# A hybrid decoder step: where one exponential stands, and which PSUM pool holds the running sums

## The chip, the cores and the metric

The kernel runs on one NeuronCore of one Trainium2 chip. The metric is the device time of one execution in microseconds (us); lower is better.

## What is computed

One inference step (512 prompt positions and 8 samples, together 520 columns) of one decoder layer with 1024 channels:

```python
x = x + 0.5 * swiglu(rmsnorm(x, norm_ffn1_w), ...)
h = rmsnorm(x); p = h @ w_in                 # z, x/B/C, dt, three short-conv parts
...
dt = softplus(dt_raw + dt_bias)
A = -exp(a_log)
a = dt * A
acum = cumsum(a, within a chunk)             # the running sums of the decays
y_ssd, S_new = ssd_scan(xs, dt, A, Bm, Cm, ssm0)
...
x = x + concat(y_ssd, y_sc) @ w_out
x = x + 0.5 * swiglu(rmsnorm(x, norm_ffn2_w), ...)
y = rmsnorm(x, final_norm_w)
```

There are 16 heads, so `a_log` holds 16 numbers; on the chip it is laid out as 128 x 16 inside the tile of small parameters `pc`.

## The kernel before

Activations lie with channels on the partitions and the 520 columns in two halves of 260. Every large product is three matmuls (high by high, high by low, low by high part); the split of a weight block into its parts is a cast on ScalarE (ACT, line 148) and a subtraction on VectorE (DVE, line 149). Weights come over SyncE's (SP's) queue into two `raw` buffers; up to four split units wait in `whl`.

The program is three stages: `ffn(1)`, `mixer`, `ffn(2)`. A scheduler of the tile framework orders each engine's instructions when the program is built; `high_priority` moves instructions forward, and the pools hand out their buffers. Nothing of that order is written out by hand.

PSUM has eight banks. In the mixer, pool `mm` holds three pairs of banks (`psum()`), used by the projections, and pool `aux` holds two single banks (`c.bank()`). The mixer begins while `ffn(1)` still ends:

- line 741: the small dt projection, into one pair of `mm` (32 matmuls);
- `nxt.factor()` (lines 304 to 314): two matmuls with ones (line 311) over the sums of squares `acc`, Sqrt on ACT (312), reciprocal on DVE (313). This gives `r`, the norm factor of all columns. The squares come from ACT (299) and are added on GpSimd (POOL, 302);
- `c.table(AF.Exp, r[:, :1])` (lines 316 to 321): a copy of one column of `r` times zero, and an exponential of it whose result is not used. ACT needs its exponential table for it (ACT_TABLE_LOAD);
- the dt chain, under `high_priority(300)`: `dth` (750), five transposes on TensorE (PE, 755), then some twenty small operations on DVE (762 to 787) with one exponential on ACT (767), which make `dt` and `da`. In between, `nega` = exp(a_log) (784), whose inputs are there from the start of the kernel;
- the running sums: matmuls at lines 791 and 792 into `pa`, a single bank, and at 805 and 806 into `ph`; copies to `acs` and `tot` (794, 795); the result goes to DRAM (`scr`, 809), from where the scan loads it (872);
- `conv(i)` for twelve blocks: `project()`, that is 48 matmuls of line 205 into a pair of `mm`, then the causal convolution on DVE and ACT (831 to 845). The scan, the short convolutions and the output projection follow.

The lines that matter, before:

```python
r = nxt.factor()
rv = halves(r)
c.table(AF.Exp, r[:, :1])
with tc.high_priority(300):
    ...
    nega = dp.tile([P, NH], F32, name="nega")
    c0 = _PC["alog"][0]
    S.activation(nega, pc[:, c0:c0 + NH], AF.Exp)
    ...
    pa = c.bank()
```

Of the kernel before, what the change touches and what calls it, by code (L numbers as in the profile page):

```python
# [10 lines left out]
F32 = mybir.dt.float32  # L11
F32R = mybir.dt.float32r
AF = mybir.ActivationFunctionType
# [3 lines left out]
P = 128  # L17
# [8 lines left out]
NH = 16  # L26
# [18 lines left out]
_PC = {}  # L45
# [10 lines left out]
def halves(ap):  # L56
    return ap.rearrange("p (h n) -> p h n", h=2)
# [14 lines left out]
class Core:  # L72
# [199 lines left out]
    def par(self, name, i, n=1):  # L272
        c = _PC[name][0] + i
        return self.pc[:, c:c + n]
# [213 lines left out]
def build(nc, tc, ctx, a, o):  # L488
# [143 lines left out]
    ffn(1, nx1, nxt)  # L632
    nx2 = Blocks(c, x, "n2", ("th", "tl", "xh", "xl"))
    mixer(c, o, x, nxt, nx2)


# [43 lines left out]
def mixer(c, o, x, nxt, nx2):  # L680
    nc, tc, a = c.nc, c.tc, c.a
    V, S, G, PE = c.V, c.S, c.G, c.PE
    par, pc = c.par, c.pc
# [8 lines left out]
    with ExitStack() as c0:  # L692
        ytp = c0.enter_context(tc.tile_pool(name="ytp", bufs=1))
        mmp = c0.enter_context(tc.tile_pool(name="mm", bufs=3, space=bass.MemoryType.PSUM))
        psum = lambda: mmp.tile([P, 2, 512], F32, tag="mm", name="mmt")
# [36 lines left out]
        with tc.tile_pool(name="dp", bufs=1) as dp:  # L732
# [11 lines left out]
            ps = ps[:, :, :H2]  # L744
            r = nxt.factor()
            rv = halves(r)
            c.table(AF.Exp, r[:, :1])
            with tc.high_priority(300):
                dth = dp.tile([NR, T], F32, name="dth")
                V.tensor_tensor(halves(dth), ps[:NR], rv[:NR], op=ALU.mult)  # L750
# [7 lines left out]
                c0 = _PC["dtb"][0]  # L758
                bias = pc[:, c0:c0 + NH]
# [19 lines left out]
                V.scalar_tensor_tensor(dt.rearrange("p c h -> p (c h)"), l1, 2.0, vf, op0=ALU.mult, op1=ALU.add)  # L779


                nega = dp.tile([P, NH], F32, name="nega")
                c0 = _PC["alog"][0]
                S.activation(nega, pc[:, c0:c0 + NH], AF.Exp)
                V.tensor_scalar(nega, nega, -1.0, None, op0=ALU.mult)
                da = dp.tile([P, NT, NH], F32, name="da")
                V.tensor_tensor(da, dt, nega.unsqueeze(1).broadcast_to([P, NT, NH]), op=ALU.mult)
                daf = da.rearrange("p c h -> p (c h)")
                NCF = NCH * NH
                pa = c.bank()  # L790
                PE.matmul(pa[:, :NCF], tri[:, 0], daf[:, :NCF], start=True, stop=True)
                PE.matmul(pa[:, NCF:2 * NCF], c.ones, daf[:, :NCF], start=True, stop=True)
                tot = dp.tile([P, NCH, NH], F32, name="tot")
# [347 lines left out]
```

## Time and profile before

| | |
|---|---|
| median of 3 runs | 1151.43 us (1151.27 to 1152.59) |
| the profiled execution | 1150.9 us, its span 1149.1 us |
| PE busy | 1118.4 us (97%) |
| PE weight loads busy | 1101.3 us (96%) |
| DVE / ACT / POOL busy | 848.4 / 539.8 / 148.6 us |
| mean granted TensorE clock | 0.99 |

The span runs from the first to the last instruction of the profiled execution, 1.8 us less than that execution's own time. Matmul records overlap, since one begins before the last has drained; the distance between starts tells the pace.

### The profile page before, as it was taken

To read this page: it belongs to the slowest core of one execution; us is meant where nothing else is said; L and a number is where in the kernel's file an instruction comes from. 1 tells how busy PE (TensorE), PEld (TensorE's weight loads), DVE (VectorE), ACT (ScalarE), POOL (GpSimd) and SP (SyncE) were. 2 spreads that over 40 slices of the span, in tenths; PEclk is the share of its full clock that TensorE was granted. 3 is DMA by queue.
4 is the path that set the end of the run, shared out by engine and by line. 5 is a ranking of instruction groups with operands and counts; after the bars stand their busy time and mean duration, and the time that the engine had idled before them with its cause. 6 is when DMAs were issued, how large, how long until landed. Compare 5 with 4: busy or idle time off the path is not lost.

```text
span 1149.1 us, 21781 instructions
## 1 busy us (share of the span) xinstructions
PE 1118.4 (97%) x9127; PEld 1101.3 (96%) x9127; DVE 848.4 (74%) x1280; ACT 539.8 (47%) x800; POOL 148.6 (13%) x247
## 2 busy tenths in 40 slices
PE   9799999999999999999999999999999999999994
PEld 8799999999999999999999999999999999999994
DVE  7788778777766675799876676349887778777755
ACT  7454434344435568466443454335544344344442
POOL 1000000000002565422221231120000000000012
PEclk9899999999999999999999999999999999999998
DMA  6123132322233523365542222331323322233223
GB/s 224 38 88 115 65 138 79 115 78 100 90 102 117 151 76 111 121 220 174 202 144 81 80 91 81 105 110 41 108 79 115 126 86 76 96 102 115 82 85 74
DMA packets 47434, 122.97 MB, mean 107 GB/s; under 512 B 9384, under 2 KB 19784, under 8 KB 41832
## 3 DMA queue, kind: packets, MB, share of 16 engines
q1 hardware_dynamic: 47336, 121.58, 32.6%
q8 instruction: 71, 1.16, 0.4%
q14 instruction: 27, 0.22, 0.1%
HBM read 114.43 MB, written 7.14 MB: 106 GB/s over the span
## 4 chain that ended last, share of the span: by engine, by line
PE 75%; DVE 11%; DMA 7%; issue 2%; ACT 2%; POOL 1%; SPq 1%; DVEq 0%; ACTq 0%; POOLq 0%
PE pst L221 30%; PE mmt L205 20%; PE auxt L582 19%; PE pst L256 4%; DMA raw<-in_wu 3%; DVE lo L149 2%; DVE st L961 1%; DMA out_ss<-st 1%; ACT hi L148 1%; DMA st<-in_ssm 1%; DVE S L134 1%; DMA raw<-in_wg 0%; DMA s<-scr 0%; DVE y L672 0%; DMA x<-in_xT 0%
## 5 line engine op out<-in xcount | busy, mean ns | idle before, releaser
L148 ACT CAST hi<-raw 128x1024 fp32r<-128x1024 f32 (+3 forms) x218 | 188.6, 869 | 288.0 <-PE mmt L205 97.7
L149 DVE TENSOR_TENSOR lo<-raw,hi 128x1024 fp32r<-128x1024 f32 (+3 forms) x218 | 219.8, 1011 | 68.8 <-ACT hi L148 65.5
L582 PE MATMUL auxt<-hh,hi 128*128 128x260 f32 x704 | 198.0, 284 | 1.7 <-DVE x L583 1.6
L582 PE MATMUL auxt<-hl,hi 128*128 128x260 f32 x704 | 197.6, 283 | 0.0
L582 PE MATMUL auxt<-hh,lo 128*128 128x260 f32 x704 | 195.1, 283 | 0.3 <-DVE lo L149 0.3
L205 PE MATMUL mmt<-xxh,hi 128*128 128x260 f32 x704 | 146.5, 288 | 0.0
L205 PE MATMUL mmt<-xxh,lo 128*128 128x260 f32 x704 | 144.5, 286 | 0.0
L205 PE MATMUL mmt<-xxl,hi 128*128 128x260 f32 x704 | 143.9, 285 | 0.0
L582 PEld LDWEIGHTS auxt<-hh,hi 128*128 128x128 f32 x704 | 132.2, 188 | 3.1 <-DVE x L583 2.4
L582 PEld LDWEIGHTS auxt<-hl,hi 128*128 128x128 f32 x704 | 132.5, 188 | 0.0
L582 PEld LDWEIGHTS auxt<-hh,lo 128*128 128x128 f32 x704 | 131.0, 188 | 0.6 <-DVE lo L149 0.5
L148 ACT CAST hi<-S 128x1024 fp32r<-128x1024 f32 x78 | 80.8, 1051 | 72.5 <-PE pst L221 43.1
L205 PEld LDWEIGHTS mmt<-xxh,hi 128*128 128x128 f32 x704 | 110.3, 191 | 0.6 <-PE auxt L909 0.2
L205 PEld LDWEIGHTS mmt<-xxl,hi 128*128 128x128 f32 x704 | 110.0, 190 | 0.8 <-issue 0.8
L205 PEld LDWEIGHTS mmt<-xxh,lo 128*128 128x128 f32 x704 | 110.0, 190 | 0.6 <-issue 0.4
L149 DVE TENSOR_TENSOR lo<-S,hi 128x1024 fp32r<-128x1024 f32 x78 | 94.5, 1220 | 16.8 <-ACT hi L148 16.6
L386 ACT ACTIVATE cp<-pst 128x260 f32<-128x260 f32 x117 | 45.0, 386 | 118.7 <-PE pst L221 118.3
L295 POOL TENSOR_TENSOR acc<-x 128x520 f32<-128x520 f32 x4 | 4.4, 1107 | 702.9 <-DVE x L583 680.1
L221 PE MATMUL pst<-fxh,hi 128*128 128x260 f32 x320 | 90.4, 284 | 0.0
L221 PE MATMUL pst<-fxl,hi 128*128 128x260 f32 x320 | 90.1, 282 | 0.0
L134 DVE TENSOR_TENSOR S<-raw 128x1024 f32<-128x1024 f32 x39 | 47.7, 1224 | 56.3 <-DMA raw<-in_wu 29.4
L221 PE MATMUL pst<-fxh,lo 128*128 128x260 f32 x320 | 89.0, 282 | 0.0
(251 smaller groups left out, 2821.2 us busy)
## 6 DMA issues: line engine op xcount, KB each, us to landing
raw<-in_wi SPq DMA_DIRECT2D x45, 512.0 KB, 3.5
raw<-in_wu SPq DMA_DIRECT2D x22, 1024.0 KB, 5.0
raw<-in_wg SPq DMA_DIRECT2D x21, 1024.0 KB, 4.9
raw<-in_wd SPq DMA_DIRECT2D x48, 384.0 KB, 3.2
raw<-in_wo SPq DMA_DIRECT2D x16, 512.0 KB, 3.7
raw<-in_wd SPq DMA_DIRECT2D x16, 256.0 KB, 2.7
st<-in_ssm SPq DMA_DIRECT2D x16, 256.0 KB, 3.5
s<-scr SPq DMA_DIRECT2D x8, 512.0 KB, 5.1
```

The source lines that it names most:

```text
L134: V.tensor_tensor(s[:, 1:3], r[:, 0:4:2], r[:, 3:4].broadcast_to([P, 2, 512]), op=ALU.add)
L148: self.S.copy(hi, src)
L149: self.V.tensor_tensor(lo, src, hi.bitcast(F32), op=ALU.subtract)
L205: self.PE.matmul(ps[:, h, :H2], w[:, k, :], x[:, h * H2:(h + 1) * H2], start=first and n == 0, stop=last and n == 2)
L221: self.PE.matmul(ps[:, :H2], a[:, k, :], b, start=first and k + i == 0, stop=k == n - 1 and i == 2, skip_group_check=True)
L256: self.PE.matmul(ps[h][:, :H2], a, b[:, h * H2:(h + 1) * H2], start=first and n == 0, stop=last and n == 2)
L295: self.G.tensor_tensor(acc, xt, xt, op=ALU.mult)
L386: self.c.S.activation(t, ps[:, :H2], AF.Copy, scale=sign)
L582: PE.matmul(ps[:, :H2], w[:, k, :], v, start=k + n == 0, stop=k == nk - 1 and n == 2)
L961: V.scalar_tensor_tensor(st[:, b], st[:, b], ddc[:, j, 1, k * HB + b:k * HB + b + 1], up[:, b], op0=ALU.mult, op1=ALU.add)
```

## The change

`nega` is computed right behind the norm factor, with a bias that is zero times the first column of `r`, and so can't start ahead of `r`. It takes the place of the dummy exponential. The two matmuls of lines 791 and 792 write into the first bank of a pair of `mm` instead of a bank of `aux`. Lines below the first edit move by up to four numbers: 755 becomes 759, 791 becomes 792, 805 becomes 806, 815 becomes 816.

```diff
             rv = halves(r)
-            c.table(AF.Exp, r[:, :1])
+
+            nega = dp.tile([P, NH], F32, name="nega")
+            zero = dp.tile([P, 1], F32, name="zero")
+            S.activation(zero, r[:, :1], AF.Copy, scale=0.0)
+            S.activation(nega, par("alog", 0, NH), AF.Exp, bias=zero)
             with tc.high_priority(300):
...
-                nega = dp.tile([P, NH], F32, name="nega")
-                c0 = _PC["alog"][0]
-                S.activation(nega, pc[:, c0:c0 + NH], AF.Exp)
                 V.tensor_scalar(nega, nega, -1.0, None, op0=ALU.mult)
...
-                pa = c.bank()
+                pa = psum()[:, 0]
                 PE.matmul(pa[:, :NCF], tri[:, 0], daf[:, :NCF], start=True, stop=True)
```

PE, before, around the matmuls of the norm factor (line 311): `mmt` is a pair of `mm`, `auxt` a bank of `aux`, `xxh` and `xxl` the parts of the normalised input.

```order
L205 MATMUL mmt<-xxh,hi 128x260
L741 MATMUL mmt<-xxl,hi 128x260 x2
L205 MATMUL mmt<-xxh,hi 128x260
L205 MATMUL mmt<-xxl,hi 128x260 x2
L311 MATMUL auxt<-acc,ones 128x260 x2
L205 MATMUL mmt<-xxh,lo 128x260 x2
```

Projections stand before and behind line 311, and go on up to the transposes of line 755 and from there to the running sums, here in the same program:

```order
L205 MATMUL mmt<-xxl,hi 128x260
L791 MATMUL auxt<-da,tri 128x64
L792 MATMUL auxt<-da,ones 128x64
L805 MATMUL auxt<-tri,da 16x256
L806 MATMUL auxt<-tri,da 16x128
L805 MATMUL auxt<-tri,da 16x256
L806 MATMUL auxt<-tri,da 16x128
L205 MATMUL mmt<-xxl,hi 128x260
```

PE in the changed program, from the end of the dt projection to the first matmul of any projection:

```order
L741 MATMUL mmt<-xxl,hi 128x260 x2
L311 MATMUL auxt<-acc,ones 128x260 x2
L759 MATMUL auxt<-idn,dth 128x48 x4
L759 MATMUL auxt<-idn,dth 8x48
L792 MATMUL mmt<-da,tri 128x64
L793 MATMUL mmt<-da,ones 128x64
L806 MATMUL auxt<-tri,da 16x256
L807 MATMUL auxt<-tri,da 16x128
L806 MATMUL auxt<-tri,da 16x256
L807 MATMUL auxt<-tri,da 16x128
L816 MATMUL auxt<-idn,dt 16x8
L205 MATMUL mmt<-xxh,hi 128x260 x2
```

Norm factor, transposes and running sums now stand one behind the other, and the first projection stands behind all of them.

ACT at the same place, before:

```order
L784 ACT_TABLE_LOAD
L784 ACTIVATE nega<-pc 128x16
L338 ACTIVATE xxh<-x_100,pc 128x520
L299 ACTIVATE sq<-x_100 128x520
L148 CAST hi<-raw 128x1024 x2
L312 ACT_TABLE_LOAD
L312 ACTIVATE r<-auxt,eps 128x260 x2
L320 ACTIVATE tbl<-r 128x1
L321 ACT_TABLE_LOAD
L321 ACTIVATE tbl<-tbl 128x1
```

and in the changed program:

```order
L338 ACTIVATE xxh<-x_100,pc 128x520
L299 ACTIVATE sq<-x_100 128x520
L148 CAST hi<-raw 128x1024
L312 ACTIVATE r<-auxt,eps 128x260 x2
L750 ACTIVATE zero<-r 128x1
L751 ACT_TABLE_LOAD
L751 ACTIVATE nega<-pc,zero 128x16
L771 ACTIVATE e<-e 128x80
L814 ACTIVATE dcs<-da 8x16
L801 ACTIVATE dec<-dec 128x64
L802 ACTIVATE cd<-cd 128x32
L148 CAST hi<-raw 128x1024
```

Two table loads and a cast are gone from ahead of the norm factor, and the exponentials of the dt chain follow it directly.

## Rows read from the trace of the kernel before

**Rows 1.** The page's first part: busy time, share of the span, instructions.

```profile
PE 1118.4 (97%) x9127; PEld 1101.3 (96%) x9127; DVE 848.4 (74%) x1280; ACT 539.8 (47%) x800; POOL 148.6 (13%) x247
```

**Rows 2.** PE's waits, whole span: total us, times, longest.

```profile
PE auxt L755 <- ACT tbl L321: 2.2, 1, 2.2
...
PE auxt L921 <- DVE xe L897: 0.8, 1, 0.8
```

**Rows 3.** Timeline of PE: start us, us, engine, line, operation [idle before].

```profile
392.18 0.40 PE L205 MATMUL mmt<-xxh,hi 128*128 128x260 f32 x2
392.42 0.40 PE L205 MATMUL mmt<-xxl,hi 128*128 128x260 f32 x2
...
396.75 0.46 PE L755 MATMUL auxt<-idn,dth 48*128 48x48 f32 x5 [2.23 <-ACT tbl L321]
397.13 0.51 PE L205 MATMUL mmt<-xxh,hi 128*128 128x260 f32 x2
```

**Rows 4.** Line 205 from 378 to 394.6 us: ns min/median/max, first and last start.

```profile
L205 PE MATMUL mmt<-xxl,hi x32: 277/282/286, 381.5 to 394.0; 128*128 128x260 f32 x32
```

**Rows 5.** Timeline of ACT, same columns as rows 3.

```profile
382.40 1.28 ACT L784 ACT_TABLE_LOAD   x1
383.70 0.22 ACT L784 ACTIVATE nega<-pc 128x16 f32<-128x16 f32 x1
383.82 0.71 ACT L338 ACTIVATE xxh<-x,pc 128x520 fp32r<-128x520 f32 x1
...
391.99 0.84 ACT L312 ACTIVATE r<-auxt,eps 128x260 f32<-128x260 f32 x2
...
409.29 0.27 ACT L767 ACTIVATE e<-e 128x80 f32<-128x80 f32 x1
```

**Rows 6.** Timeline: POOL's last sum of squares, and PE's norm factor.

```profile
385.14 1.36 POOL L302 TENSOR_TENSOR acc<-acc,sq 128x520 f32<-128x520 f32 x1 [3.53 <-ACT sq L299]
...
387.47 1.04 PE L311 MATMUL auxt<-acc,ones 128*128 128x260 f32 x4
```

**Rows 7.** Timeline of DVE, from the last split ahead of the norm factor.

```profile
390.71 1.22 DVE L149 TENSOR_TENSOR lo<-raw,hi 128x1024 fp32r<-128x1024 f32 x1 [1.08 <-ACT hi L148]
392.50 3.42 DVE L313 RECIPROCAL r<-r 128x260 f32<-128x260 f32 x2 [0.56 <-ACT r L312]
395.95 0.69 DVE L750 TENSOR_TENSOR dth<-mmt,r 48x520 f32<-48x520 f32 x1
...
410.98 0.64 DVE L770 RECIPROCAL q<-q 128x80 f32<-128x80 f32 x1
...
418.16 0.50 DVE L776 SCALAR_TENSOR_TENSOR l<-l,q 128x80 f32<-128x80 f32 x2
```

**Rows 8.** Timeline of PE at the running sums.

```profile
422.19 0.43 PE L791 MATMUL auxt<-da,tri 128*128 128x64 f32 x2
...
424.19 0.39 PE L205 MATMUL mmt<-xxl,hi 128*128 128x260 f32 x1
```

**Rows 9.** Timeline of PE behind its longest pause, in the first FFN.

```profile
35.91 0.56 PE L256 MATMUL pst<-xxh,hi 128*128 128x260 f32 x1 [5.77 <-DVE g L427]
36.26 0.42 PE L256 MATMUL pst<-xxl,hi 128*128 128x260 f32 x1
36.48 0.42 PE L256 MATMUL pst<-xxh,lo 128*128 128x260 f32 x1
```

**Rows 10.** Stretches: us, busy of PE, PEld, DVE, ACT, POOL; PEclk, DMA share, GB/s.

```profile
33.00:34.00 1.00, 0.00 (x0) 0.00 (x0) 1.00 (x2) 0.00 (x0) 0.00 (x0) 0.59 0.00 0
39.00:40.00 1.00, 1.00 (x7) 1.00 (x6) 0.91 (x3) 0.00 (x0) 0.00 (x0) 0.50 0.00 0
40.00:41.00 1.00, 1.00 (x10) 1.00 (x10) 0.10 (x1) 0.00 (x0) 0.00 (x0) 1.00 0.00 0
390.00:405.00 15.00, 12.77 (x96) 12.49 (x95) 12.47 (x19) 7.50 (x11) 8.54 (x11) 0.89 0.33 108
420.00:440.00 20.00, 20.00 (x149) 18.80 (x148) 13.85 (x28) 15.80 (x25) 12.82 (x29) 0.91 0.42 134
470.00:640.00 170.00, 168.32 (x1392) 160.44 (x1391) 140.17 (x254) 86.15 (x176) 38.91 (x75) 1.00 0.49 159
```

**Rows 11.** ACT's waits for the scan's loads: total us, times, longest.

```profile
ACT s L880 <- DMA s<-scr: 17.1, 5, 5.9
```

## The prediction

> **What bounds the kernel now.** I read the page's engine line first. PE is busy 97% of the span and its weight loads 96%, DVE 74%, ACT 47% [rows 1]: matmuls set the time, and a change moves it by what it adds to or takes from PE's idle time and PE's clock. PE's list of waits came next. Around this change it has one wait of weight, 2.2 us at the transposes of line 755 [rows 2]. In the timeline PE is idle for 2.23 us before them, and a matmul of line 205 follows at 397.13, at the transposes' heels [rows 3]. That matmul needs nothing of what the transposes waited for, yet it did not run in the pause. So PE takes matmuls in their order, and what stands behind a waiting one waits too. Last came the order of the instructions before and after, because the cost of the pause depends on what stands behind it.
>
> Before, projections fill almost all of the time in which ACT, POOL and DVE make the norm factor and the dt chain. Between 378 and 394.6 us line 205 issues three products with 32 matmuls each, one of them shown [rows 4]: 96, which is conv blocks one and two whole. In the changed order every one of these stands behind the running sums. I take the reason to be the second edit: the pair for `pa` is asked for ahead of the pairs of the conv blocks, and the pool serves requests in program order. The order is a fact; its reason is not needed for the sum.
>
> **The first edit, step by step.** The exponential of `a_log` leaves the place where it had its own table load, 1.28 us with 0.1 us more until `xxh` began [rows 5]. The reload for Sqrt and the reload behind it become one load behind the norm factor. So the chain to the norm factor shortens. `xxh` can start at 382.4 instead of 383.8, and POOL's last addition, which started 1.32 us behind `xxh`, at 383.7; it ends 1.36 us later, at 385.1 [rows 5, 6]. The matmuls of line 311, which queued behind projections until 387.47, start at 385.2 and are through 1.04 us later, at 386.2 [rows 6].
>
> From there, on the profile's clock:
> - the two square roots without a load, 0.84 us [rows 5]: about 386.0 to 386.9. DVE first finishes a split of 1.22 us [rows 7] whose cast waits for the end of the dt projection (about 384.9): it ends at 387.2.
> - the two reciprocals, 3.42 us [rows 7]: 390.6. `nega` on ACT needs the first of them (388.9), a copy of 0.2, the load of 1.28 and 0.22 [rows 5]: 390.7, and its negation on DVE some 0.2 us. It now stands ahead of `dth`, but ends almost with the second reciprocal. I charge 0.3 us.
> - `dth`, 0.69 us [rows 7]: 391.6. The transposes begin 0.1 us later and take 0.46 us [rows 3]: 392.2.
> - the dt chain with nothing between its steps. Five small operations, one exponential of 0.27 us [rows 5], one reciprocal of 0.64 us, and thirteen dependent steps at 0.25 us, the pace of the pair at line 776 [rows 7]. With 1.0 us for the first five and 0.1 for two hand-overs: 1.0 + 0.4 + 0.6 + 3.3 = 5.3 us. `da` is ready at 397.5.
>
> **The second edit.** PE reaches the running sums at 397.5 with all work done except those 96 matmuls. Before, it was at the same point, behind the transposes, at about 397.2, with the 96 done. At 0.12 us each (two in 0.24 us [rows 3]) they are worth 11.5 us; with the 0.3 us the delay is **11.8 us**. Seen the other way, PE idles some 14 us between 381.4 and 397.5, against 2.2 us before. No other work covers it. Bounds: 10.8 if the split and `nega` cost nothing, 13.3 if each small step takes 0.06 us more and the matmuls of line 311 run at half pace.
>
> The clock. Behind a pause of 5.77 us the matmuls came 0.22 us apart [rows 9]; the granted clock stood at half (1.2 GHz) from within the pause, 33.4, until 40.0, 4.1 us after the work came back [rows 10]. So each microsecond at half loses 0.45 us. Before, a share of 0.89 in 15 us and of 0.91 in 20 us [rows 10] are 3.3 and 3.6 us at half, 1.5 us lost each: one behind the 2.2 us pause, one behind the 16-column matmuls of line 821. After, PE comes back from a longer pause at half. The running sums, 2.0 us at full pace [rows 8], lose between 0 and 2.0; I take 1.0, the middle, since small matmuls are only partly paced by the clock. The projections behind them lose 0.5 (if 4.1 us count from the running sums) to 1.8 (if from the first projection): 1.2. The fall behind line 822 stays at 1.5, or melts into the first. Sum 3.7 against 3.0: **+0.7**, bounds -1.5 and +3.8 (the upper with one more stretch of 1.5).
>
> Costless edits. The two matmuls of the running sums have the same shape in either bank. The other table loads that go (ten fewer in the whole program) lie on ACT, which PE doesn't wait for there. SP now holds the store of the sums and two scan loads ahead of most `in_wi` loads, but four split units are in hand when the pause begins, 23 us of PE's work at 5.76 us each; if that cover failed, PE would wait for a weight load. The scan's inputs are ready far earlier; PE's waits in the scan's stretch are only 1.7 us of 170 [rows 10], so between 0 and 1.6 us can come back. I take 0.
>
> Sum: 11.8 + 0.7 = +12.5 us on the profiled execution's own 1150.9, so 1163.4. The median of the runs is 0.5 us above that execution: **1164 us**.
>
> A price where row and notes part: the load that leaves the path is 1.28 us, and the next operation starts 0.02 us behind it [rows 5]. The Trainium skill (ScalarE: Activation LUTs, What ACT_TABLE_LOAD costs) gives 2.66 us for a switch, half of it a drain that these rows don't show. By it the chain would be 1.4 us shorter and the sum an estimated 11.1.
>
> **The rivals.**
> 1. *PE is not held up: faster.* The new order's chain would run beside projections, the 2.2 us pause at line 755 would go, and with it the half clock behind it, 1.5 us: 1151.4 - 3.7 = 1147.7. For it: the pause is put down to ACT's dummy exponential [rows 2], and ACT's chain gets shorter by two loads. Against it: this needs a projection ahead of the running sums on PE, and the new order has none. It decides as soon as 12 us of projections can pass. 3%. The Trainium skill's rule to group activations by table set (ScalarE: Activation LUTs, Table sets: the hidden batching unit) speaks for this side; the trace agrees that each set change has its load, but it has them on an engine that is 47% busy.
> 2. *A second pause in the conv stage.* ACT now has scan operations, which wait for loads from `scr` of up to 5.9 us [rows 11], ahead of the first block's convolution; DVE's evacuation of the third block needs that block's buffer, and the three pairs of PSUM run dry. Price up to 5.9 us: 1170. It decides if ACT is late by more than two blocks of projection, 11.5 us; I find about 3 us. 8%.
> 3. *The delay is partly given back*: chain at its lower bound, the scan's 1.6 us returned, no second fall of the clock: 10.8 - 1.5 - 1.6 = +7.7, 1159. 8%.
> 4. *No change at the end*: the order is as shown, but PE's pause had been paid elsewhere before. PE's busy share leaves no such place. 2%.
>
> **How the numbers follow.** The forecast has 79%. The range takes its bounds, without their coinciding extremes, and most of rival 3: 1160 to 1168. Left out are rival 1, rival 4, most of rival 2 and the extreme of rival 3, below 2 in 10 together. A measurement of this kernel can tell about 0.2%, 2.3 us, from no change. Faster by more than that is rival 1, 0.03; within it rival 4, 0.02; slower all else, 0.95.
>
> **What would show it.** In the changed kernel's timeline PE should stand still three times: about 3 us in pieces before line 311, some 5.5 us from there to the transposes at line 759, some 5.3 us from there to line 792. Its waits should name DVE's `dth` or `nega` and DVE's `da`. The granted clock should be at half when line 792 starts and for some 3 to 6 us on. The first `L205` with `mmt` should start near 400. The dt chain from `dth` to `da` should take about 6 us, against 26. From there on every line should lie some 12.5 us later than before, with no new wait. A projection between lines 311 and 792 on the timeline, or a PE pause in the conv stage, would prove me wrong.

## The result, and the profile after

| | before | after |
|---|---|---|
| median of the runs | 1151.70 us (1151.27 to 1152.59, 4 runs) | 1161.67 us (1161.11 to 1163.64, 4 runs) |
| ratio of after to before | | 1.0092, 95% interval 1.0076 to 1.0109 |
| the profiled execution, its span | 1150.9 us, 1149.1 us | 1163.64 us, 1161.8 us |
| mean granted TensorE clock | 0.990 | 0.984 |

The change makes the kernel slower by 10.0 us between the medians; 1164 us had been forecast. The profiled execution of after is the slowest of its four, 2 us above their median. So a second profile of the same kernel (after_again, below) stands beside it where the two differ.

The page of after, first part, against [rows 1]: the engines' work is nearly the same, the span is not.

```profile
PE 1120.3 (96%) x9127; PEld 1101.8 (95%) x9127; DVE 853.2 (73%) x1280; ACT 527.9 (45%) x789; POOL 145.1 (12%) x247
```

PE's waits in the whole span of after (line, what it waited for: total us, times, longest), against [rows 2]:

```profile
PE mmt L792 <- DVE da L788: 5.6, 1, 5.6
...
PE auxt L759 <- issue: 5.0, 1, 5.0
PE auxt L865 <- DVE sn L927: 1.8, 1, 1.8
...
PE mmt L741 <- ACT xxh L338: 1.2, 1, 1.2
...
PE mmt L741 <- DVE xxl L339: 0.8, 1, 0.8
PE auxt L311 <- POOL acc L302: 0.6, 1, 0.6
```

Those of lines 741, 311, 759 and 792 stand in one place; line 759 is line 755 of before, whose 2.2 us have become 5.0, and the others are new there. At line 759 the profile finds no releaser (`issue`); DVE's `dth` ends at 392.78 us (its row is below), 0.1 us ahead of the transposes, which read it. PE's timeline of after (columns as in rows 3), against [rows 3] and [rows 8]:

```profile
383.38 0.51 PE L741 MATMUL mmt<-xxh,hi 128*128 128x260 f32 x2 [1.17 <-ACT xxh L338]
384.68 0.51 PE L741 MATMUL mmt<-xxl,hi 128*128 128x260 f32 x2 [0.79 <-DVE xxl L339]
385.82 2.10 PE L311 MATMUL auxt<-acc,ones 128*128 128x260 f32 x4 [0.64 <-POOL acc L302]
392.88 0.71 PE L759 MATMUL auxt<-idn,dth 48*128 48x48 f32 x5 [4.96 <-issue]
399.19 0.69 PE L792 MATMUL mmt<-da,tri 128*128 128x64 f32 x2 [5.61 <-DVE da L788]
...
403.02 0.80 PE L205 MATMUL mmt<-xxh,hi 128*128 128x260 f32 x2
```

PE stands still for 1.17 + 0.79 + 0.64 + 4.96 + 5.61 = 13.2 us between 382 and 399 us, against 2.23 us before [rows 3]: 10.9 us more, with not one projection of line 205 in between. The first projection comes at 403.02, behind the running sums.

DVE's timeline of after, the chain in these pauses, against [rows 7]:

```profile
386.30 1.23 DVE L149 TENSOR_TENSOR lo<-raw,hi 128x1024 fp32r<-128x1024 f32 x1 [1.67 <-ACT hi L148]
387.60 3.42 DVE L313 RECIPROCAL r<-r 128x260 f32<-128x260 f32 x2
391.27 0.91 DVE L786 TENSOR_SCALAR nega<-nega 128x16 f32<-128x16 f32 x1 [0.25 <-ACT nega L751]
392.10 0.68 DVE L754 TENSOR_TENSOR dth<-mmt,r 48x520 f32<-48x520 f32 x1
...
398.90 0.24 DVE L788 TENSOR_TENSOR da<-dt,nega 128x80 f32<-128x80 f32 x1
```

The dt chain, from the start of `dth` to the end of `da`, takes 392.10 to 399.14, 7.0 us, where DVE has nothing else to do; before it ran from 395.95 [rows 7] until the running sums at 422.19 [rows 8].

Stretches of after (us, busy of PE, PEld, DVE, ACT, POOL; PEclk, DMA share, GB/s), against [rows 10]:

```profile
381.00:386.00 5.00, 2.40 (x16) 1.77 (x15) 2.30 (x4) 2.98 (x4) 2.53 (x5) 0.91 0.96 201
386.00:392.00 6.00, 1.92 (x4) 0.99 (x4) 5.37 (x4) 3.02 (x6) 4.35 (x11) 0.50 0.73 266
...
405.00:406.00 1.00, 1.00 (x7) 1.00 (x8) 0.00 (x0) 0.00 (x0) 0.00 (x0) 0.71 0.00 0
406.00:481.50 75.50, 75.50 (x629) 75.33 (x628) 48.97 (x61) 40.97 (x60) 47.66 (x114) 1.00 0.31 94
```

The clock is at half (1.2 GHz) from within the pauses to 405.6 us. From 406 us to the scan's first matmul at 481.50 PE works without a gap and at full pace. The 16-column matmuls of line 822 stand in this stretch, at 407.80, and no fall of the clock follows them here, as one did behind line 821 before (the 0.91 of [rows 10]).

### The profile page after: what moved, and what is told of

It is laid out like the page before. It is cut to its first block, busy times and chain, and to the rows that moved or that the text cites. A ratio compares the mean times of both kernels' runs of the same rounds, so it can differ in the third digit from the quotient of the medians.

```text
span 1161.8 us, 21776 instructions
## 1 busy us (share of the span) xinstructions
PE 1120.3 (96%) x9127; PEld 1101.8 (95%) x9127; DVE 853.2 (73%) x1280; ACT 527.9 (45%) x789; POOL 145.1 (12%) x247
## 4 chain that ended last, share of the span: by engine, by line
PE 80%; DVE 9%; DMA 7%; ACT 2%; issue 2%; POOL 0%; SPq 0%; DVEq 0%; ACTq 0%; POOLq 0%
PE pst L221 31%; PE mmt L205 22%; PE auxt L582 19%; PE pst L256 4%; DVE lo L149 2%; DMA raw<-in_wu 2%; DMA out_ss<-st 1%; DMA s<-scr 1%; DVE st L962 1%; DMA raw<-in_wg 1%; DMA st<-in_ssm 1%; ACT hi L148 1%; DVE S L134 1%; DVE y L672 0%; POOL acc L302 0%
```

## Experiments

The theory: the second edit asks for a pair of `mm` ahead of the conv blocks, so in program order ahead of their pairs; the pool serves in that order, and the scheduler can no longer put the two blocks' 96 projections ahead of the running sums. PE has nothing to do while ACT, POOL and DVE make the norm factor and the dt chain. The rivals: it is the first edit, by a longer chain; or it is the use of a pair of `mm` for the sums, whoever asks for it.

**One edit alone.** e1_exp_only keeps the exponential's new place and gives `pa` back its bank of `aux`:

```diff
-                pa = psum()[:, 0]
+                pa = c.bank()
```

> Only the first edit: the exponential of a_log behind the norm factor, the running sums in a bank of aux as before. Theory (the pair requested ahead of the conv blocks' pairs holds the projections back): projections stay between line 311 and the running sums, no pause of 5 us on PE. Two table loads less ahead of the norm factor (2 x 1.28 us), so the transposes of line 759 are ready about when PE reaches them: the pause of 2.2 us and the half clock behind it (1.5 us) go, about 1148 us, ratio 0.997, range 0.995 to 1.001. Rival (the exponential's new place with high priority pulls the dt chain forward): as the changed kernel, 1161 to 1164, ratio 1.009.

Measured: 1150.74 us median of 11 runs, ratio to before 0.9994 (0.9980 to 1.0009). No slowdown. PE's timeline has the projections ahead of the transposes again, and a shorter pause than the 2.23 us of [rows 3]:

```profile
394.72 0.41 PE L205 MATMUL mmt<-xxh,lo 128*128 128x260 f32 x2
396.32 0.46 PE L759 MATMUL auxt<-idn,dth 48*128 48x48 f32 x5 [1.19 <-ACT hi L148]
```

The gain that was expected did not reach the end. The first operation of the scan on DVE (the row of its group: ns min/median/max, first and last start) comes at 470.0 us before and at 468.4 here:

```profile
L976 DVE TENSOR_TENSOR t<-mmt,xs x8: 692/699/711, 470.0 to 619.1; 128x520 f32<-128x520 f32 x8
```

```profile
L977 DVE TENSOR_TENSOR t<-mmt,xs x8: 692/695/700, 468.4 to 620.3; 128x520 f32<-128x520 f32 x8
```

The last of these eight starts 1.2 us later than before. In between PE waits for DVE 4.6 us, against 1.7 us of idle time in the scan before [rows 10]:

```profile
PE auxt L865 <- DVE sn L927: 1.8, 1, 1.8
PE auxt L922 <- DVE xe L898: 1.7, 1, 1.7
...
PE auxt L910 <- DVE xd L897: 1.1, 2, 0.7
```

The first FFN happens to end 0.6 us later in this execution than before (the last matmul of line 582 starts at 381.76 and 381.13 us), so the conv stage itself gained some 2.2 us, and the scan took 2.8 back. Why DVE is later there was not tried.

e2_bank_only is the other half: the kernel before with only the pair for `pa`.

```diff
-                pa = c.bank()
+                pa = psum()[:, 0]
```

> Only the second edit: the running sums in a pair of mm, the exponential of a_log and the dummy exponential as before. Theory: the projections stand behind the running sums, as in the changed kernel, and the chain is longer by the early table load and the Sqrt load (1.28 us each, partly beside a split): 1162 to 1166, ratio 1.010 to 1.013, three pauses of PE that add up to 14 to 17 us. Rival (the exponential's place does it): within 0.2% of before, 1149 to 1154.

Measured: 1162.33 us median of 4 runs, ratio 1.0107 (1.0088 to 1.0126). The whole slowdown is there, with the dummy exponential still in place. PE's waits:

```profile
PE mmt L791 <- DVE da L787: 5.6, 1, 5.6
PE auxt L755 <- ACT tbl L321: 4.8, 1, 4.8
PE mmt L741 <- ACT xxh L338: 2.7, 1, 2.7
```

The two long pauses are those of after. With the short ones the pauses add up to 13.7 us, just under the 14 to 17 expected. The wait for `xxh` is 2.7 us, where after has 1.2; with the two short ones behind it (0.29 and 0.34 us here) the stretch ahead of line 311 costs 3.3 us against 2.6: that 0.7 us is what the first edit takes out of the way in this order. The profiled execution, 1159.36 us, is the fastest of the four, and its first FFN ends 2.1 us earlier than before (line 582: 379.05 and 381.13 us); from there to the scan's first matmul it takes 13.7 us longer than before.

**A pair, but no new request.** e3_own_pair has both edits, but `pa` lies in the pair that the dt projection already holds:

```diff
+            pw = ps
             ps = ps[:, :, :H2]
...
-                pa = psum()[:, 0]
+                pa = pw[:, 0]
```

> Both edits, but the running sums go into the first bank of the pair that the dt projection already has, so no new pair is requested; that pair is held longer, until tot is copied. Theory (it is the request, in program order): as with the first edit alone, about 1148, ratio 0.995 to 1.001. Rival (it is that a pair of mm holds the running sums, so that one pair less is left for the projections): a pause where the third conv block needs that pair, or the changed order: 1155 to 1164.

Measured: 1150.38 us median of 12 runs, ratio 0.9999 (0.9988 to 1.0009). The running sums write into banks of `mm` and nothing is lost: 96 projections stand ahead of the transposes again, whose pause is 1.2 us. It is the request in its place in the program, not the pool that the sums use.

**The same kernel again.** after_again is the changed kernel once more.

> The changed kernel once more. The record's profiled execution took 1163.6 us and its median was 1161.7; both theories expect the median again, 1161 to 1162.5, ratio 1.008 to 1.010. Open: whether the 1.8 us wait of line 865 on DVE (0.3 before) is in this profile too; if it is only an execution's own, the scan stage starts and ends at the same distance from before, some 11 us.

Measured: 1161.31 us median of 4 runs, ratio 1.0095 (1.0079 to 1.0110). The pauses of lines 759 and 792 are again 5.0 and 5.6 us. The clock is not the same in detail:

```profile
401.00:402.00 1.00, 1.00 (x6) 0.38 (x4) 0.04 (x1) 0.00 (x0) 0.00 (x0) 0.65 0.00 0
402.00:403.00 1.00, 1.00 (x9) 0.84 (x8) 0.64 (x1) 0.00 (x0) 0.00 (x0) 1.00 0.00 0
408.00:409.00 1.00, 1.00 (x9) 1.00 (x8) 0.00 (x0) 0.00 (x0) 0.00 (x0) 0.77 0.26 10
409.00:411.00 2.00, 2.00 (x11) 2.00 (x11) 0.00 (x0) 0.00 (x0) 0.00 (x0) 0.50 0.99 321
411.00:412.00 1.00, 1.00 (x7) 1.00 (x6) 0.28 (x1) 0.71 (x1) 0.00 (x0) 0.53 1.06 219
```

Here it is back at full (2.4 GHz) at 401.7 us, before the first projection, but falls once more from 408.5 to 411.9, behind the 16-column matmuls of line 822. The wait of 1.8 us at line 865 is not there: PE's waits in the scan are 0.3 and 0.2 us. So it comes in some profiles and not in others (that of e1_exp_only has it too), and it makes up most of the first profile's distance to the median.

**Conv blocks ahead of the request.** In e8_conv2_ahead and e8_conv4_ahead the changed kernel's `conv` stands ahead of the dt chain, and two or four blocks are called before `pa` asks for its pair:

```diff
                 V.tensor_tensor(da, dt, nega.unsqueeze(1).broadcast_to([P, NT, NH]), op=ALU.mult)
+            for i in (8, 9, 10, 11)[:AHEAD]:
+                conv(i)
+            with tc.high_priority(300):
                 daf = da.rearrange("p c h -> p (c h)")
...
-        for i in [8, 9, 10, 11] + list(range(8)):
+        for i in [8, 9, 10, 11][AHEAD:] + list(range(8)):
```

> The changed kernel with the first two conv blocks standing in program order ahead of the request for the pair of the running sums; the running sums still go into a pair of mm. By its order PE has 96 projections ahead of the transposes again, but none between the transposes and the running sums, and DVE has two blocks of convolution (about 8 us) inside the dt chain. Theory (PE idles for whatever the chain takes beyond the projections that were requested ahead of the pair): almost no pause at the transposes, one of 9 to 12 us at the running sums, ratio 1.007 to 1.011. Rival (the cost is the chain with nothing done meanwhile, so 96 matmuls returned are 11.5 us returned): within 0.2% of before.

Measured: 1160.04 us median of 4 runs, ratio 1.0097 (1.0077 to 1.0117). The order follows the requests as the theory says: 96 projections are back ahead of the transposes, whose pause is 1.2 us. But the time stays lost, in one pause at the running sums:

```profile
394.85 0.46 PE L783 MATMUL auxt<-idn,dth 48*128 48x48 f32 x5 [1.18 <-ACT hi L149]
409.53 0.66 PE L819 MATMUL mmt<-da,tri 128*128 128x64 f32 x2 [14.22 <-issue]
```

The pause was expected 9 to 12 us long and is longer, because the conv blocks' own work now stands inside the dt chain. The largest piece is on DVE, where six steps of the convolution (line 745) and a split stand among the chain's small steps: from the transposes at 394.85 to the end of `e` (line 794) at 401.64 it takes 6.8 us, where after takes 1.8.

```profile
401.42 0.22 DVE L794 SCALAR_TENSOR_TENSOR e<-v 128x80 f32<-128x80 f32 x1
```

The other piece is on ACT, two loads and a SiLU ahead of the chain's exponential of line 795, which starts 3.3 us behind the end of `e`, where after has 0.04:

```profile
400.90 1.28 ACT L754 ACT_TABLE_LOAD   x1 [3.94 <-DVE cv L745]
402.28 1.37 ACT L754 ACTIVATE xs<-cv 128x520 f32<-128x520 f32 x2
403.67 1.28 ACT L795 ACT_TABLE_LOAD   x1
404.96 0.27 ACT L795 ACTIVATE e<-e 128x80 f32<-128x80 f32 x1
```

> The same with four conv blocks ahead of the request. PE's order has 96 more projections between the transposes and the running sums (11.5 us). Theory: the pause at the running sums shrinks to 3 to 7 us, ratio 1.002 to 1.006. Rival: as with two blocks, whatever that gives, since the pair itself is still taken from the projections.

Measured: 1157.51 us median of 4 runs, ratio 1.0066 (1.0050 to 1.0081). The pause at the running sums falls to 9.7 us, not to the 3 to 7 expected, and the ratio lies just above the expected range: 96 more projections fill 11.5 us of PE, but line 819 starts 7.7 us later than with two blocks (417.25 and 409.53), since the further convolutions lengthen the chain too. Both expectations were wrong in size, with the direction right.

**The chain's terms.** The forecast gave the negation of `nega` 0.3 us of path; DVE's timeline of after shows 0.91 us and 0.25 of waiting ahead of it. e9_after_fold takes the instruction out and folds the sign into `da`:

```diff
-                V.tensor_scalar(nega, nega, -1.0, None, op0=ALU.mult)
...
-                V.tensor_tensor(da, dt, nega.unsqueeze(1).broadcast_to([P, NT, NH]), op=ALU.mult)
+                V.scalar_tensor_tensor(da, dt, -1.0, nega.unsqueeze(1).broadcast_to([P, NT, NH]), op0=ALU.mult, op1=ALU.mult)
```

> The changed kernel with the negation of nega folded into the product that makes da (one operation of DVE less, and dth no longer stands behind it). It measures the term that the prediction put at 0.3 us; in the profile the negation started 0.25 us late and took 0.91 us ahead of dth. Theory: dth 1.0 to 1.2 us earlier, PE's pause before the transposes 4.0 instead of 5.0 us, 1 us less in time: ratio 1.008. Rival (the transposes wait for something else): no change of that pause, ratio 1.009 to 1.0095.

Measured: 1159.73 us median of 6 runs, ratio 1.0084 (1.0067 to 1.0101). The pause before the transposes is 4.0 us in place of 5.0: 1 us, as expected. The two ratios differ by 0.0008, 0.9 us, well inside their intervals: the gain can be read from the trace, not from the times. `dth` starts as soon as the second reciprocal is done:

```profile
386.61 3.42 DVE L313 RECIPROCAL r<-r 128x260 f32<-128x260 f32 x2
390.13 0.69 DVE L754 TENSOR_TENSOR dth<-mmt,r 48x520 f32<-48x520 f32 x1
```

Why the negation is that long, e10_sq_on_act asks. In after it ends with POOL's multiplication of line 755 (391.10 to 392.15 us). The experiment gives that multiplication to ACT; the orders of PE and DVE stay.

```diff
-                G.tensor_tensor(rr, r, r, op=ALU.mult)
+                S.activation(rr, r, AF.Square)
```

> The changed kernel with one instruction moved: the square of the norm factor at line 755 goes from POOL to ACT, behind the exponential of a_log; PE's and DVE's orders stay as they are. Question: why the 128x16 negation at line 786 takes 0.91 us where it took 0.17 us before. Theory: it waits while POOL's multiplication of 128x520 at line 755 runs (391.10 to 392.15; the negation ends at 392.18). Then without that POOL operation the negation takes 0.17 to 0.2 us, dth starts some 0.75 us earlier, PE's pause before the transposes falls from 5.0 to 4.2 us, and the time by about 0.8 us. Rival: the negation is slow by itself there, because its input has just been written by ACT or because DVE has been idle: then it stays at 0.9 us, the pause at 5.0 us and the time at 1161.5 us.

Measured: 1159.11 us median of 4 runs, ratio 1.0081 (1.0064 to 1.0097). The negation is back at 0.17 us:

```profile
385.48 3.41 DVE L313 RECIPROCAL r<-r 128x260 f32<-128x260 f32 x2
389.14 0.17 DVE L786 TENSOR_SCALAR nega<-nega 128x16 f32<-128x16 f32 x1 [0.25 <-ACT nega L751]
389.22 0.69 DVE L754 TENSOR_TENSOR dth<-mmt,r 48x520 f32<-48x520 f32 x1
```

From the start of the reciprocals to the transposes it takes 4.53 us (385.48 to 390.01) against 5.28 in after (387.60 to 392.88): the 0.75 us expected. PE's pause itself falls only to 4.8 us, since line 311 ran 1.39 us in this profile, not 2.10, and so the pause began earlier. The ratio lies 0.0011 below that of after, 1.3 us, and the intervals overlap: the 0.8 us can be read from the trace, not from the times.

**A version that beats both.** b1_exp_fold is e1_exp_only with the fold of e9_after_fold: `pa` in its bank of `aux`, the exponential in its new place, no negation.

> The first edit alone, with the negation folded in the same way. In the run of the first edit alone PE paused 1.2 us at the transposes, where dth stood behind the negation and so behind ACT's exponential; here dth needs the reciprocals only. Theory: that pause goes or falls below 0.3 us, so conv stage 1 us earlier; but the scan stage took back what the first edit gained, and its DVE is as full as before, so ratio 0.996 to 1.001. Rival (the scan's pauses in that run were its own execution's): the gain stays, ratio 0.995 to 0.997.

Measured: 1147.58 us median of 12 runs, ratio to before 0.9978 (0.9967 to 0.9989). The pause before the transposes is all but gone, and the scan begins 3.0 us earlier than before:

```profile
394.54 0.46 PE L759 MATMUL auxt<-idn,dth 48*128 48x48 f32 x5 [0.21 <-issue]
```

```profile
L976 DVE TENSOR_TENSOR t<-mmt,xs x8: 685/694/701, 467.0 to 618.0; 128x520 f32<-128x520 f32 x8
```

The last of the eight starts 1.1 us earlier than before: the scan takes 1.9 us back, as in e1_exp_only, but here a part stays, 0.2% of the time.

## Why the prediction was right, and what was mis-sized

- **The place and the reason.** 96 projections stand behind the running sums, and PE idles through the norm factor and the dt chain. e2_bank_only shows that the second edit alone does it, e3_own_pair that it is the request's place in the program, e8_conv2_ahead that requests moved ahead bring their projections ahead.
- **The signs.** The three pauses were forecast at some 3, 5.5 and 5.3 us; they measured 2.6 (1.17 + 0.79 + 0.64), 5.0 and 5.6. The dt chain took 7.0 us where some 6 were forecast. The first projection came at 403.0 us, in after_again at 402.0, where near 400 was forecast. The clock stood at half for 6.4 and 3.5 us from the start of line 792, against 3 to 6.
- **The sum up to the scan.** Forecast 11.8 for the delay at the running sums and 0.7 for the clock, 12.5. PE sets the time, so the stage is read from PE's own rows: from the last matmul of the first FFN (line 582) to the first of the scan, in before, after and after_again:

```profile
381.13 0.28 PE L582 MATMUL auxt<-hh,lo 128*128 128x260 f32 x1
468.18 0.60 PE L858 MATMUL auxt<-xs 128*128 128x256 f32 x2
```

```profile
381.45 0.28 PE L582 MATMUL auxt<-hh,lo 128*128 128x260 f32 x1
481.50 0.60 PE L859 MATMUL auxt<-xs 128*128 128x256 f32 x2
```

```profile
380.47 0.28 PE L582 MATMUL auxt<-hh,lo 128*128 128x260 f32 x1
480.89 0.60 PE L859 MATMUL auxt<-xs 128*128 128x256 f32 x2
```

  That is 87.05, 100.05 and 100.42 us, so 13.0 and 13.4 more than before. Of this 0.24 us are two of the 96 projections, which before stood ahead of the first mark: the change costs 12.8 and 13.1 us here. (DVE's first operation in the scan is no good mark for it: before, it ran 1.8 us behind line 858, in after 0.3 behind line 859; in e1_exp_only and b1_exp_fold 1.9 and 2.1, so there it serves.) The idle time makes up 13.17 - 2.23 = 10.9, where 14 - 2.2 was forecast; the rest is PE's own work, which takes longer.
- **The 11.8 was some 1.1 us too small.** Line 792 starts at 399.19; before, PE was behind the transposes at 397.2 [rows 3]. That is 2.0 us later, with the 96 matmuls (11.5 us) still to do. Of it 0.6 us are the first FFN's, whose work the change leaves as it is: it ends 0.3 us later, though the two projections (0.24 us) no longer stand in it. So the delay is 2.0 - 0.6 + 11.5 = 12.9 us, between the forecast and its upper bound of 13.3. In after_again line 792 starts at 398.22 and the FFN is 0.4 us quicker: 12.9 again.
- **Inside the chain.** Counted from the first FFN's end, line 792 comes 1.4 us later than the 397.5 forecast. Some 0.1 us came up to the end of the reciprocals. 0.8 us came from `nega`: `dth` starts 1.1 us behind the reciprocals, not 0.3, and in e9_after_fold 0.1. 0.5 us came from the transposes to `da`, 6.3 us for the 5.8 forecast. Two other terms were mis-sized at almost no cost: POOL's last addition took 1.83 us, not 1.36, and line 311 2.10 us at half pace, not 1.04. The reciprocals wait for DVE's split as well, which ends at 387.53; they start at 387.60. In e10_sq_on_act, where line 311 took only 1.39 us, they start 1.62 us behind its start, in after 1.78: 0.71 us less on PE gave 0.16.
- **The clock's 0.7 was 0.5 to 0.7 us too large.** The running sums lost more than the 1.0 taken: from line 792 to the first projection 403.02 - 399.19 = 3.8 us, 3.7 in after_again, against the 2.0 of [rows 8]. So these small matmuls ran at almost half their pace; that they are "only partly paced by the clock" didn't hold. The projections behind them ran at half until 405.6 us in after, 2.6 us at a loss of 0.45 each, 1.2 us as taken; in after_again they lost nothing. The fall behind line 822 melted into the first in after; in after_again it came separately, for 3.4 us, a loss of 1.5. That makes 3.0 and 3.2 us against the 3.0 before: 0.0 and 0.2, where 0.7 was forecast. With the delay these are 12.9 and 13.1 us, against the 12.8 and 13.1 of the marks. (The clock of [rows 10] falls at 33.2, not at 33.4; no term hangs on it.)
- **From the scan to the end** 0 was taken. The span is 12.7 us longer in after and 10.6 in after_again (1159.7 us), and the scan's first matmul comes 13.3 and 12.7 later: 0.6 and 2.1 us came back. PE's waits in the scan are 2.3 us in after and 0.5 in after_again, in place of 1.7 [rows 10]; behind the scan another 1.0 and 0.9 us came back, and why is open. The give-back of rival 3 is thus there in part.
- **What was luck.** The place, the cause and the sign were argued and are shown. That the forecast lies only 2.3 us above the median is in part luck: the delay was taken too small, the clock too large, and a give-back was left out that more than makes up for the rest.
- **The rivals.** PE was held up (rival 1). No pause came in the conv stage (rival 2): PE is busy 75.50 of the 75.50 us from 406 to 481.5, and ACT waited only 0.26 us for the scan's load, as its timeline shows:

```profile
413.56 1.28 ACT L881 ACTIVATE s<-s,acs 128x128 f32<-128x128 f32 x4 [0.26 <-DMA s<-scr]
```

  The cover for the weight loads held too: PE waits for nothing in this stretch.
- **The price of a table load.** In after the load at 389.63 us takes 1.28 us and the exponential follows at 390.93:

```profile
389.63 1.28 ACT L751 ACT_TABLE_LOAD   x1
390.93 0.31 ACT L751 ACTIVATE nega<-pc,zero 128x16 f32<-128x16 f32 x1
```

  The sum's 1.28 holds. The 2.66 us of the Trainium skill (ScalarE: Activation LUTs, What ACT_TABLE_LOAD costs) shows nowhere on this path.

## What to carry to other kernels

A request to a pool is an order: a buffer asked for early in the program can hold back all that asks the same pool later, however urgent or free of data dependencies that is. So compare the order on the bound engine first, and price what no longer stands in its pauses; here 96 matmuls of 0.12 us set the sign, and the table loads saved on ACT could not. Saved waits can also come back further down, where another engine is nearly full: read a landmark at the end of each stage, on the engine that sets the time, and not only the pause that went.

## What the hardware showed beyond what was expected

- A DVE operation of 128x16 that takes 0.17 us took 0.91 us (1.01 in e1_exp_only) while POOL multiplied 128x520, and ended with it; with POOL's multiplication moved to ACT it took 0.17 again (e10_sq_on_act). DVE's `dth` beside the same POOL operation took its usual 0.69 us (e9_after_fold, 390.13 us; POOL from 390.11 for 1.05). The Trainium skill (GPSIMD Engine Reference, Key points) says that POOL shares its SBUF interfaces with VectorE and contends with some forms of its instructions only; both rows fit that, though no row shows which form the 128x16 operation had.
- The clock came back at different points behind the same pauses: at 405.6 us, 6.4 us behind the start of line 792, in after, and at 401.7, 3.5 us behind it, in after_again. The sooner return was followed by another fall at 408.5.
